# A seventh product taken in quarters, with eleven small sums on GpSimd, two passing weight quarters by DMA and half of C scaled last, in a Strassen matmul on one core

## The chip, the core and the metric

The kernel runs on one core of one Trainium2 chip. The metric is the device time of one execution in microseconds; the time before is the median of three runs, 1456.64 us (1456.58 to 1457.28). The profiled execution that the views come from has a span of 1455.0 us from its first to its last instruction.

## What is computed

```python
cs = np.cumsum(x, axis=1)                       # x: 8 x 2048 x 2048, w: 2048 x 2048, float32
diff = cs - np.concatenate([zeros, cs[:, :-1, :]], axis=1)
return np.matmul(diff, w)
```

The running sum and the difference undo each other, so the result is x times w: 16384 rows, in 128 row tiles of 128, by 2048 columns.

## The kernel before

**Stages.** Row tiles 0 to 3 are done plainly while w arrives (lines 180 to 457). Tiles 4 to 7 (`group_plain`, L628) and 8 to 11 (`group_half`, L752) lead over to the steady part: 29 groups of four row tiles, g, h, k and l (class `Group`, L957), from tile 12 on. A group multiplies its four tiles with all of w by a Winograd form of Strassen's scheme: the four tiles make a 2 x 2 block of A (rows g, h above k, l; each tile has a left and a right half of the inner dimension), w a 2 x 2 block of B, and seven products P1 to P7 give the four blocks of C. Weights stay in SBUF as f16, with their sums T1 to T4 (`T3 = B22 - B12`).

**Products.** P1 to P5 are each taken by the same scheme a second time, as seven quarter products p1 to p7: a quarter is four matmuls of 128 x 512 (L573), so such a product is 28 matmuls. P6 (S2 x T2) and P7 (S3 x T3) are taken whole, by `whole` (L1182) and `steps` (L547), 32 matmuls each at L554. A group is 5 x 28 + 2 x 32 = 204 matmuls.

**What surrounds a quarter product.** Four small sums of x halves per product, s1 to s4 (`small_sums`, L1001, `total` at L544, 128 x 512 f16 on VectorE; s1 feeds s2, s2 feeds s4). Eight sums S1 to S4 of whole tiles (128 x 1024, L544 too). Some weight quarters have no place in SBUF and pass through one buffer, `flow`: `fill_by` (L934) has VectorE compute a quarter (128 x 2048 f16, L937) just before the product that reads it, six times a group (P1.fp4, P2.fp4, P3.fp2, P4.fp4, P5.fp4, P5.fp5). PSUM has eight banks; `copy` (L1023, ScalarE) and `merge` (L1030, VectorE, `PSUM bank = PSUM bank + c`) carry a partial sum from one bank to others.

**C.** Each result piece of 128 x 512 f32 is started in an SBUF buffer c (seven of them, list `free`) by `keep` (L581, ScalarE: `c = bank * unit`) and completed by `add` (L584, VectorE: `c = bank * unit + c`), then stored by `put` (L595, a DMA of SyncE). A group has 16 keeps, 26 adds and 16 puts.

**x.** A row tile is loaded in two halves (L111), its absolute sum taken (`weigh`, ScalarE, L123), turned into a scale and its inverse (`scale_of`, VectorE, L139 and L141; `unit_of`, GpSimd, L147, 128 x 1), narrowed to f16 in place (L158, ScalarE) and transposed by DMA (L171). Left halves rotate through three buffers `F[:, 0..2]`, right halves through two.

**Order.** Every instruction is put behind the one before it on its engine (`after`, L86), and the order is written out in `ORDER` (L1195): one round of 188 steps for a group in the steady state, where `+1` and `+2` mean steps of the next groups. So each engine works through its own steps strictly in the order of that text. `END_ORDER` (L1227) orders P4 of the last group.

Of the kernel before, what the change touches and what calls it, by code (L numbers as in the profile page):

```python
# [10 lines left out]
def kernel(  # L11
# [86 lines left out]
    for t in range(PLAIN + 4, END, 4):  # L98
        queue_of_x += [t, t + 2, t + 1, t + 3]
    for i, t in enumerate(queue_of_x):  # L100
        where[t] = [F[:, i % 3, :], F[:, 3 + i % 2, :]]
# [30 lines left out]
    def scale_of(t):  # L132
        if t < END:
# [6 lines left out]
            )  # L140
            after("dve", lambda: nc.vector.reciprocal(s, m))  # L141
            sizes[t] = m

    def unit_of(t):
        if t < END:
            u, m = unit[t], sizes.pop(t)
            after("pool", lambda: nc.gpsimd.tensor_scalar(u, m, uw, None, MUL))  # L147
# [346 lines left out]
    class Inner:  # L494
# [20 lines left out]
        def weights(self):  # L515
# [4 lines left out]
            return {j: pieces_of(t) for j, t in places.items()}  # L520
# [10 lines left out]
    def half_of(t, i):  # L531
        return in_twos(t)[:, i]
# [10 lines left out]
    def total(dst, p, q, op):  # L543
        after("dve", lambda: nc.vector.tensor_tensor(dst.all, p.all, q.all, op))  # L544
# [389 lines left out]
    def fill_by(op, a, b):  # L934
        def some():
            x, y = (in_twos(t) for t in (a, b))
            after("dve", lambda: nc.vector.tensor_tensor(in_twos(flow), x, y, op))  # L937

        return some

    sevens = {
        "P1": (in_1, {"p4": fill_by(SUB, quarter_of(0, 1, 0), S1_all)}),
        "P2": (in_2, {"p4": fill_by(SUB, quarter_of(4, 1, 0), inner[:, 8:12, :])}),
        "P3": (in_3, {"p2": fill_by(ADD, spare_of(2, 0), inner[:, 16:20, :])}),
        "P4": (in_4, {"p4": fill_by(SUB, quarter_of(7, 1, 0), spare_of(2, 4))}),
# [3 lines left out]
                "p4": fill_by(SUB, quarter_of(1, 1, 0), quarter_of(6, 1, 0)),  # L949
                "p5": fill_by(SUB, quarter_of(1, 1, 1), quarter_of(6, 1, 0)),  # L950
# [5 lines left out]

    class Group:  # L957
        def __init__(self, g):
            self.tiles = dict(g=g, h=g + 2, k=g + 1, l=g + 3)
# [26 lines left out]
        def quarter(self, P, j, b, fresh):  # L986
# [4 lines left out]
            def some():  # L991
                to, a = self.bank(b, fresh), self.sums[P][j]
                quarter(
                    to, self.real(a), passed if j in passes else inner.weights()[j], fresh
                )
# [5 lines left out]
        def small_sums(self, P, a, b, dead, places=()):  # L1001
# [5 lines left out]
            def one(j, p, q, op):  # L1007
                if isinstance(to[j], str):
                    self.take(to[j], scratch)
                total(self.real(to[j]), self.real(p), self.real(q), op)  # L1010
# [37 lines left out]

        def row(self, c):
            return self.tiles[c[3] if c[1] == "1" else {"g": "k", "h": "l"}[c[3]]]  # L1050

        def keep(self, c, b, let=False):
            def some():
                keep(self.take(c, free), self.at[b], unit[self.row(c)])
# [231 lines left out]
```

## Time and profile before

| | before |
|---|---|
| median of runs | 1456.64 us |
| span of the profiled execution | 1455.0 us |
| busy: PE / VectorE (DVE) / ScalarE (ACT) / GpSimd (POOL) | 1441.1 / 1333.3 / 967.5 / 48.6 us |
| one group in the steady state | 44.03 us |
| DVE, ACT and POOL busy in it | 40.78, 29.6 and 1.07 us |

The runs' time has 1.6 us around the span. A busy time is the union of an engine's instructions, so where two of them overlap by their ends it is less than the sum of their durations. PE is matmul, PEld weight loads (beside PE), SP is SyncE, whose queue issues all DMAs of the steady part. A releaser ("<-") is what an engine's idle time before an instruction ended with.

### The profile page before, as it was taken

What the parts mean: (1) busy time and instruction counts of PE and PEld (TensorE: products, weight loads), DVE (VectorE), ACT (ScalarE), POOL (GpSimd) and SP (SyncE); (2) the same over time, 40 slices, a digit from 0 to 9 for tenths busy, and PEclk for the clock granted to TensorE, in tenths of its full rate; (3) what the DMA queues carried; (4) which work ended last, traced back from release to release, by engine and by line L of the source; (5) the groups of instructions that cost most, each with busy time, mean ns of one, the idle gap of its engine ahead of it and who ended that gap; (6) DMA issues with size and microseconds to landing.
All of it is one profiled execution on the core that took longest, in us unless ns stands there. A gap on an engine that the chain in (4) does not pass through costs nothing.

```text
span 1455.0 us, 20120 instructions
## 1 busy us (share of the span) xinstructions
PE 1441.1 (99%) x6673; PEld 652.6 (45%) x6679; DVE 1333.3 (92%) x2302; ACT 967.5 (66%) x1446; POOL 48.6 (3%) x136
## 2 busy tenths in 40 slices
PE   8999999999999999999999999999999999999998
PEld 3444444444444444444444444444444444444443
DVE  7998899999999999999999999999999999999998
ACT  5887656676666666667666667766666766666662
POOL 0111000000000000000000000000000000000000
PEclk9999999999999999999999999999999999999999
DMA  9999868898888998878998888998878898888983
GB/s 360 367 240 299 236 171 234 248 246 232 234 237 237 248 253 230 235 236 233 260 241 233 231 228 240 260 238 241 225 235 247 247 233 239 226 244 246 253 203 123
DMA packets 377752, 351.59 MB, mean 242 GB/s; under 512 B 274800, under 2 KB 274800, under 8 KB 377520
## 3 DMA queue, kind: packets, MB, share of 16 engines
q1 hardware_dynamic: 377088, 348.47, 84.9%
q0 software_dynamic: 560, 1.84, 0.3%
q8 instruction: 52, 0.85, 0.2%
q14 instruction: 52, 0.43, 0.1%
HBM read 150.99 MB, written 134.22 MB: 196 GB/s over the span
## 4 chain that ended last, share of the span: by engine, by line
PE 96%; DMA 2%; DVE 1%; issue 0%; ACT 0%; SPq 0%; DVEq 0%; ACTq 0%
PE b L573 61%; PE b L554 32%; PE b L275 2%; DMA W<-in_w_dram 1%; DMA W<-in_x_dram 1%; DVE c L584 1%; ACT wb L259 0%; PE b L400 0%; DVE x L544 0%; SPq L219 0%; DVE b L1030 0%; DVE flow L937 0%; DVE inner L544 0%; DVE W L541 0%; ACT c L581 0%
## 5 line engine op out<-in xcount | busy, mean ns | idle before, releaser
L584 DVE SCALAR_TENSOR_TENSOR c<-b,of,c 128x512 f32<-128x512 f32 x790 | 574.1, 747 | 74.3 <-PE b L573 64.3
L554 PE MATMUL b<-W,x 128*128 128x512 f16 x2144 | 506.6, 379 | 0.0
L581 ACT ACTIVATE c<-b,of 128x512 f32<-128x512 f32 x492 | 312.6, 680 | 230.9 <-PE b L573 113.3
L573 PE MATMUL b<-W,x 128*128 128x512 f16 x1892 | 452.4, 379 | 0.8 <-ACT b L1023 0.7
L158 ACT ACTIVATE F<-F,of 128x1024 f16<-128x1024 f32 x246 | 282.2, 1147 | 174.8 <-DVE of L141 172.6
L573 PEld LDWEIGHTS <-x 128*128 128x128 f16 x2488 | 243.4, 98 | 295.3 <-issue 2.7
L554 PEld LDWEIGHTS <-x 128*128 128x128 f16 x2144 | 209.8, 98 | 253.0 <-DVE x L544 0.2
L123 ACT ACTIVATE waste<-F 128x1024 uint8<-128x1024 f32 x246 | 259.3, 1054 | 4.6 <-DMA F<-in_x_dram 2.5
L573 PEld LDWEIGHTS <-inner 128*128 128x128 f16 x1648 | 161.2, 98 | 195.6 <-issue 1.3
L573 PE MATMUL b<-W,inner 128*128 128x512 f16 x944 | 242.2, 379 | 0.9 <-DVE b L1030 0.9
L544 DVE TENSOR_TENSOR x<-x,x 128x1024 f16<-128x1024 f16 (+1 forms) x388 | 226.6, 584 | 3.3
L573 PE MATMUL b<-flow,x 128*128 128x512 f16 x588 | 150.9, 379 | 0.0
L573 PE MATMUL b<-inner 128*128 128x512 f16 x472 | 121.1, 379 | 0.0
L937 DVE TENSOR_TENSOR flow<-W 128x2048 f16<-128x2048 f16 x87 | 105.8, 1216 | 0.0
L1030 DVE TENSOR_TENSOR b<-b,c 128x512 f32<-128x512 f32 x116 | 80.6, 695 | 13.9 <-PE b L573 13.9
L147 POOL TENSOR_SCALAR of<-of,uw 128x1 f32<-128x1 f32 x124 | 43.6, 370 | 1306.7 <-DVE of L139 704.1
L937 DVE TENSOR_TENSOR flow<-W,inner 128x2048 f16<-128x2048 f16 x58 | 70.8, 1220 | 0.0
L1023 ACT COPY c<-b 128x512 f32<-128x512 f32 x58 | 33.4, 576 | 51.3 <-PE b L573 51.3
L275 PE MATMUL b<-wb,xP 128*128 128x512 bf16 x234 | 57.0, 395 | 5.3 <-ACT wb L259 3.9
L544 DVE TENSOR_TENSOR inner<-x 128x512 f16<-128x512 f16 x117 | 49.4, 422 | 2.9 <-DMA x<-F 0.9
L1023 ACT COPY b<-b 128x512 f32<-128x512 f32 x87 | 51.2, 588 | 0.5 <-PE b L573 0.5
L544 DVE TENSOR_TENSOR inner<-x,inner 128x512 f16<-128x512 f16 x117 | 49.2, 421 | 2.0
(67 smaller groups left out, 530.0 us busy)
## 6 DMA issues: line engine op xcount, KB each, us to landing
F<-in_x_dram SPq DMA_DIRECT2D x246, 512.0 KB, 5.1
out_dram<-c SPq DMA_DIRECT2D x492, 256.0 KB, 3.0
W<-in_w_dram SPq DMA_DIRECT2D x32, 512.0 KB, 9.6
W<-in_x_dram SPq DMA_DIRECT2D x16, 256.0 KB, 7.2
x<-F SPq DMA_TRANSPOSE x246, 3.4
out_dram<-o POOLq DMA_DIRECT2D x5, 256.0 KB, 4.1
out_dram<-o SPq DMA_DIRECT2D x5, 256.0 KB, 3.5
xP<-in_x_dram SPq DMA_DIRECT2D x1, 1024.0 KB, 5.1
```

Of the source, the lines that this page charges most:

```text
L123: lambda: nc.scalar.activation(waste, where[t][i], ABS, scale=1.0 / ROW, accum_out=sums_of[t][:, i : i + 1],),
L147: after("pool", lambda: nc.gpsimd.tensor_scalar(u, m, uw, None, MUL))
L158: lambda: nc.scalar.activation(narrowed(t)[:, ds(i * NH, NH)], where[t][i], COPY, scale=s),
L275: lambda: nc.tensor.matmul(ps[r][n], xP[:, r, ko, :], wb[h, ko][:, ds(n * NB, NB)], start=(ko == 0), stop=(ko == KO - 1),),
L544: after("dve", lambda: nc.vector.tensor_tensor(dst.all, p.all, q.all, op))
L554: said = nc.tensor.matmul(to[n], a[k], b[k][:, n, :], start=(first and k == 0), stop=(k == KH - 1), skip_group_check=True,)
L573: said = nc.tensor.matmul(to, a[k], b[k], start=(first and k == 0), stop=(k == 3), skip_group_check=True)
L581: after("act", lambda: nc.scalar.activation(c, p, COPY, scale=u))
L584: after("dve", lambda: nc.vector.scalar_tensor_tensor(c, p, u, c, MUL, ADD))
L937: after("dve", lambda: nc.vector.tensor_tensor(in_twos(flow), x, y, op))
L1023: after("act", lambda: nc.scalar.copy(c, p))
L1030: after("dve", lambda: nc.vector.tensor_tensor(t, p, s, ADD))
```

## The change

- **P7 by seven quarter products** (`onto`), on top of what P6 left in the four banks x: four copies (c1, c5, c6, c7) on ScalarE and six merges (a1, a5g, a5h, a6, a7h, a7k) on VectorE take its partial sums to the banks, three of its weight quarters pass by fills (P7.fp4, P7.fp5, P7.fp7), and it has four small sums. T3's own quarters are rewritten once at the start (`sums_of_T3`).
- **Eleven of the now 24 small sums** go to GpSimd (`ON_POOL`).
- **Two of the now nine fills** (P1.fp4 and P5.fp5) are computed once by VectorE, stored to a DRAM tile and from the next group on loaded from there by a DMA of SyncE (class `Fill`), into the third left buffer of x, which the x tiles give up after the first eleven.
- **Eight of 16 result pieces** (`LATE`; not in the last group) are kept without their factor, added as a plain tensor_tensor, and scaled in place at the end by ScalarE (`last.*`).
- The reciprocal is a step of its own (`recip`), and `ORDER` is a new text.

```diff
+    THREE = 11
     for i, t in enumerate(queue_of_x):
-        where[t] = [F[:, i % 3, :], F[:, 3 + i % 2, :]]
+        j = i % 3 if i < THREE else (i - THREE) % 2
+        where[t] = [F[:, j, :], F[:, 3 + i % 2, :]]
...
+    ON_POOL = "P1.s1 P1.s4 P2.s1 P2.s2 P2.s3 P3.s2 P3.s3 P4.s2 P4.s3 P4.s4 P5.s2".split()
+    def total(dst, p, q, op, pool=False):
+        if pool:
+            after("pool", lambda: nc.gpsimd.tensor_tensor(dst.all, p.all, q.all, op))
+        else:
+            after("dve", lambda: nc.vector.tensor_tensor(dst.all, p.all, q.all, op))
...
+    flows = [flow, F[:, 2, :].bitcast(f16).rearrange("p (k n) -> p k n", k=4)]
+    class Fill:
+        def __call__(self):
+            if self.again is not None:
+                after("sp", lambda: nc.sync.dma_start(self.to, self.again))
+                return
+            x, y = (in_twos(t) for t in (self.a, self.b))
+            after("dve", lambda: nc.vector.tensor_tensor(in_twos(self.to), x, y, self.op))
+            if self.can:
+                self.again = kept.tile([P, 4, NB], f16, name=f"kept{len(stored)}")
+                stored.append(self)
+                after("sp", lambda: nc.sync.dma_start(self.again, self.to))
...
+        "P7": (
+            in_7,
+            {
+                "p4": Fill(SUB, quarter_of(5, 1, 0), quarter_of(5, 0, 1)),
+                "p5": Fill(SUB, quarter_of(5, 1, 1), quarter_of(5, 0, 1)),
+                "p7": Fill(SUB, quarter_of(5, 0, 1), quarter_of(5, 0, 0)),
+            },
+        ),
...
+    LATE = 'C12g0 C12g1 C12h1 C12h0 C11g1 C11h1 C21g1 C21h1'.split()
...
+        def onto(self, P, h0, h1, g0, g1):
+            q, e = f"{P}q", f"{P}e"
+            self.quarter(P, "p1", q, True)
+            self.step(f"{P}.c1", snap(f"{P}1", q))
+            self.merge(f"{P}.a1", g0, g0, f"{P}1", let=True)
+            self.quarter(P, "p2", g0, False)
+            self.quarter(P, "p5", e, True)
+            self.step(f"{P}.c5", snap(f"{P}5", e, True))
+            self.merge(f"{P}.a5g", g1, g1, f"{P}5")
+            self.merge(f"{P}.a5h", h1, h1, f"{P}5", let=True)
+            self.quarter(P, "p3", g1, False)
+            self.quarter(P, "p6", q, False)
+            self.step(f"{P}.c6", snap(f"{P}6", q))
+            self.merge(f"{P}.a6", g1, g1, f"{P}6", let=True)
+            self.quarter(P, "p7", q, False)
+            self.step(f"{P}.c7", snap(f"{P}7", q, True))
+            self.merge(f"{P}.a7h", h1, h1, f"{P}7")
+            self.merge(f"{P}.a7k", h0, h0, f"{P}7", let=True)
+            self.quarter(P, "p4", h0, False)
...
         def keep(self, c, b, let=False):
+                if c in self.late:
+                    after("act", lambda: nc.scalar.copy(to, p))
+                else:
+                    keep(to, p, u)
         def add(self, c, b, tag, let=False):
+                if c in self.late:
+                    after("dve", lambda: nc.vector.tensor_tensor(to, p, to, ADD))
+                else:
+                    add(to, p, u)
         def put(self, c):
+            if c in self.late:
+                self.step(f"last.{c}", lambda: keep(self.at[c], self.at[c], unit[self.row(c)]))
...
-            self.whole("P7", T3, half["g"][0], half["h"][0], *x)
+            self.small_sums("P7", A("g", 0), A("h", 0), True)
+            self.onto("P7", *x)
...
+    ORDER = """
+    P5.p7+0 P5.m2+0 P4.p2+0 P3.p6+0 keep.C22h1+0 P3.s3+0 P5.p3+0 put.C22g0+0 P5.fp4+0
+    P5.p4+0 add.C12h1.z+0 scale.h+1 add.C12g1.q+0 keep.C12h0+0 keep.C22h0+0 P7.a7k+0
+    P4.p1+0 recip.h+1 P4.s1+0 P7.fp4+0 keep.C21g0+0 P3.p7+0 turn1.g+1 put.C12g0+0
+    add.C21g0.x+0 P4.s3+0 P3.p4+0 P7.p4+0 P1.fp4+1 P1.p1+1 load.k+1 add.C12h1.q+0
+    narrow0.h+1 keep.C22g1+0 add.C12h0.z+0 add.C22g1.x+0 P3.p3+0 turn0.h+1 unit.g+1
+    P4.s2+0 add.C12h0.q+0 add.C22h0.x+0 add.C12g1.z+0 narrow1.h+1 P1.cg+1 turn1.h+1
+    P4.p6+0 last.C12h0+0 weigh0.k+1 P4.fp4+0 weigh1.k+1 P4.s4+0 add.C22h1.x+0 scale.k+1
+    recip.k+1 P3.p5+0 add.C12g1.e+0 put.C22h0+0 P4.p5+0 P4.p3+0 P1.p2+1 narrow0.k+1
+    P1.s1+1 add.C12h1.e+0 P1.s2+1 P4.p4+0 P1.p5+1 P1.s3+1 last.C12h1+0 keep.C21h1+0
+    put.C21g0+0 put.C22g1+0 keep.C21g1+0 put.C12h0+0 P1.s4+1 P1.ct+1 P1.p6+1 P2.p1+1
+    add.C21h1.e+0 add.C21g1.q+0 put.C22h1+0 narrow1.k+1 P1.m1+1 add.C21g1.x+0 P2.s1+1
+    P2.s2+1 load.l+1 keep.C11g0+1 unit.h+1 P2.cv+1 turn0.k+1 P4.p7+0 add.C21h1.q+0
+    last.C12g1+0 P2.fp4+1 P1.p7+1 P2.s4+1 P1.p3+1 P2.p2+1 P1.m2+1 P2.s3+1 P2.p6+1
+    weigh0.l+1 P1.p4+1 keep.C11g1+1 weigh1.l+1 add.C11g0.v+1 keep.C21h0+0 add.C11g1.q+1
+    scale.l+1 recip.l+1 narrow0.l+1 P2.p5+1 turn1.k+1 S1.g+1 narrow1.l+1 put.C11g0+1
+    S2.g+1 P2.p7+1 add.C21h0.x+0 put.C12g1+0 keep.C11h1+1 add.C11h1.q+1 P5.p1+1
+    turn0.l+1 last.C21g1+0 P6g.0+1 P6g.3+1 add.C11h1.e+1 S4.g+1 turn1.l+1 P2.p4+1
+    keep.C11h0+1 add.C11h0.q+1 P5.cg+1 P3.fp2+1 put.C21g1+0 last.C11h1+1 P6g.2+1
+    last.C21h1+0 S1.h+1 S2.h+1 P5.p2+1 put.C21h0+0 unit.k+1 P6g.1+1 P2.p3+1 put.C12h1+0
+    load.g+2 put.C21h1+0 keep.C22g0+1 keep.C12g0+1 S3.g+1 S4.h+1 P5.s1+1 P5.s2+1 P3.p2+1
+    add.C11g1.e+1 add.C12g0.z+1 last.C11g1+1 P6h.1+1 P5.s3+1 P6h.0+1 P6h.3+1 P5.s4+1
+    weigh0.g+2 P6h.2+1 weigh1.g+2 P5.fp5+1 P7.p1+1 P7.c1+1 P7.fp5+1 S3.h+1 P7.s1+1
+    put.C11h0+1 scale.g+2 P7.s3+1 recip.g+2 narrow0.g+2 keep.C12g1+1 P5.p6+1 P7.a1+1
+    P7.s2+1 P7.p5+1 P7.c5+1 P7.fp7+1 P7.s4+1 P5.p5+1 put.C11h1+1 put.C11g1+1 P7.a5g+1
+    P3.s1+1 P7.p6+1 P7.p2+1 keep.C12h1+1 P7.c6+1 P7.p7+1 unit.l+1 P7.a6+1 P5.ct+1
+    load.h+2 P7.a5h+1 turn0.g+2 P7.p3+1 add.C22g0.x+1 P3.s2+1 P7.c7+1 narrow1.g+2
+    P3.p1+1 P5.m1+1 P3.s4+1 weigh0.h+2 P7.a7h+1 add.C12g0.q+1 last.C12g0+1 weigh1.h+2
+    """
+    def sums_of_T3():
+        less(in_7.t12, in_7.t12, in_7.t11)
+        less(in_7.Q2, in_7.t22, in_7.t12)
```

95 lines of the change are left out of this document (43 added, 52 removed).

## The prediction

> **What bounds the kernel now.** I read the page first (busy times and the chain that ended last), then the table by windows for two rounds of the steady part, then the chain in order of time, then the groups.
>
> ```profile
> PE 1441.1 (99%) x6673; PEld 652.6 (45%) x6679; DVE 1333.3 (92%) x2302; ACT 967.5 (66%) x1446; POOL 48.6 (3%) x136
> ...
> PE 96%; DMA 2%; DVE 1%; issue 0%; ACT 0%; SPq 0%; DVEq 0%; ACTq 0%
> ```
>
> ```profile
> core 0: us, PE busy (x) PEld busy (x) DVE busy (x) ACT busy (x) POOL busy (x), PEclk, DMA share, GB/s
> ...
> 822.63:866.66 44.03, 44.03 (x206) 19.98 (x204) 40.78 (x72) 29.60 (x46) 1.07 (x4) 1.00 0.87 238
> ...
> 1350.99:1395.02 44.03, 44.03 (x206) 19.95 (x204) 40.79 (x72) 29.61 (x46) 1.07 (x4) 1.00 0.89 239
> ```
>
> ```profile
> 1350.99 18.13 PE b L573 x84
> ...
> 1395.02 18.13 PE b L573 x84
> ```
>
> The chain is matmul for 96% of the span. Equal places of two rounds lie 44.03 us apart (1350.99 and 1395.02), 84 matmuls in a row take 18.13 us, so one takes 0.2158 us, and the group's 204 matmuls take 204 x 0.2158 = 44.03 us: PE loses nothing in a round. The granted clock is 1.00, so there is nothing to win from it. Next comes VectorE with 40.78 us of 44.03, 93%; 3.25 us of its round are idle. ScalarE has 14.4 us free and GpSimd 43.
>
> What ends VectorE's idle time in that round, from the list of waits of 822.63 to 866.66:
>
> ```profile
> ACT F L158 <- DVE of L141: 5.9, 3, 2.8
> ...
> DVE c L584 <- PE b L573: 2.1, 5, 0.8
> ...
> DVE b L1030 <- PE b L573: 0.5, 1, 0.5
> ```
>
> 2.6 of its 3.25 us are waits for PE: VectorE had caught up with the matmuls. Such idle time is slack, and it shrinks by itself when VectorE has more to do. The 5.9 us in which ScalarE's narrowing waits for the reciprocal (L141) is a block at the head of an engine that works in order.
>
> **The change, part by part.**
>
> *Matmuls.* P7 goes from 32 to 28, a group from 204 to 200: 200 x 0.2158 = 43.16 us, 0.863 less. 29 groups: **-25.0 us**. That is certain as work and is also the most that can be won: 1455.0 - 25.0 = 1430.0 us of span. The median of the runs is 1.6 us above the span, so 1431.6.
>
> *VectorE's work per group.* The prices, from the groups by shape, and below them the same instructions in order of time:
>
> ```profile
> L584 DVE SCALAR_TENSOR_TENSOR c<-b,of,c 128x512 f32<-128x512 f32 x790 | 574.1, 747 | 74.3 <-PE b L573 64.3 <-ACT c L581 1.3
> ...
> L937 DVE TENSOR_TENSOR flow<-W 128x2048 f16<-128x2048 f16 x87 | 105.8, 1216 | 0.0
> L1030 DVE TENSOR_TENSOR b<-b,c 128x512 f32<-128x512 f32 x116 | 80.6, 695 | 13.9 <-PE b L573 13.9
> ...
> L544 DVE TENSOR_TENSOR inner<-x 128x512 f16<-128x512 f16 x117 | 49.4, 422 | 2.9 <-DMA x<-F 0.9
> ```
>
> ```profile
> 834.63 0.74 DVE L584 SCALAR_TENSOR_TENSOR c<-b,of,c 128x512 f32<-128x512 f32 x1
> 835.29 0.69 DVE L1030 TENSOR_TENSOR b<-b,c 128x512 f32<-128x512 f32 x1
> 835.89 1.22 DVE L937 TENSOR_TENSOR flow<-W,S 128x2048 f16<-128x2048 f16 x1
> 837.02 0.42 DVE L544 TENSOR_TENSOR inner<-x 128x512 f16<-128x512 f16 x1
> 837.48 0.42 DVE L544 TENSOR_TENSOR inner<-inner,x 128x512 f16<-128x512 f16 x1
> 837.82 0.69 DVE L1030 TENSOR_TENSOR b<-b,c 128x512 f32<-128x512 f32 x1
> ```
>
> The starts show what an instruction really takes from the round, since its end lies over the next one: an add 835.29 - 834.63 = 0.66, a merge 0.60, a fill 1.13, a small sum 0.34 (837.48 to 837.82) to 0.46 when the next one needs it (837.02 to 837.48), 0.40 on average. I use these, and the full durations as the other end:
> - six merges more: 6 x 0.60 = +3.6 (full: 6 x 0.695 = +4.2)
> - fills 6 to 7 (nine, less two by DMA): +1.13 (+1.22)
> - small sums 20 to 13 (24, less eleven): -7 x 0.40 = -2.8 (-2.95)
> - 18 of the 26 adds belong to late pieces and become plain tensor_tensor. The trace has that form only into PSUM, the merge: -18 x 0.06 = -1.1 if it costs the same into SBUF, 0 if it costs what the add does. I take -1.0, since the merge has the same operation and the same two kinds of input.
>
> Sum +0.9, so **41.7 us** busy in a round of 43.16 (41.2 with the other ends in its favour, 43.3 with all against, just over the matmuls): 97%, with 1.5 us free instead of 3.25. Without the three parts that take work off VectorE (GpSimd, DMA, late scaling) it would be 41.7 + 11 x 0.40 + 2 x 1.13 + 1.0 = 49.4, and VectorE the bound by far.
>
> *ScalarE.* Four copies more, and eight scalings of a c; the eight late keeps become copies. From the groups:
>
> ```profile
> L581 ACT ACTIVATE c<-b,of 128x512 f32<-128x512 f32 x492 | 312.6, 680 | 230.9 <-PE b L573 113.3 <-issue 63.2 <-PE b L554 28.6
> ...
> L1023 ACT COPY c<-b 128x512 f32<-128x512 f32 x58 | 33.4, 576 | 51.3 <-PE b L573 51.3
> ```
>
> +4 x 0.58 + 8 x 0.68 - 8 x 0.10 = +6.9 us: 36.5 of 43.16, 85%. It hides beside the matmuls, but a late scaling waits for VectorE's last add, and what stands behind it on ScalarE waits too: behind `last.C12h1` stand keep.C21h1, keep.C21g1 and P1.ct, and P1.ct feeds the merge P1.m1. 6.6 us of free time has to cover such blocks and the 5.9 us of the reciprocal's.
>
> *GpSimd.* Eleven sums of 128 x 512. No instruction of the trace shows that size on GpSimd; these are the bounds:
>
> ```profile
> 78.86 1.36 POOL L147 TENSOR_SCALAR of<-of,uw 128x1 f32<-128x1 f32 x1 [4.79 <-DVE of L139]
> ...
> 116.86 0.28 POOL L147 TENSOR_SCALAR of<-of,uw 128x1 f32<-128x1 f32 x1 [5.01 <-DVE of L139]
> ...
> 139.70 1.90 POOL L147 TENSOR_SCALAR of<-of,uw 128x1 f32<-128x1 f32 x1 [16.29 <-DVE of L139]
> ```
>
> Between 0.28 us (128 x 1) and 1.90 us (the longest GpSimd instruction beside VectorE's work). I take the upper one, as the work is 512 times that of the row: 11 x 1.9 = 21 us of 43, still half free. The four `unit` steps queue behind the sums and have no waiter in the list of waits. What counts is not GpSimd's time but what its sums do to VectorE, below. The Trainium skill, "GPSIMD Engine Reference", section "3.1 Elementwise — side-by-side cycle accounting", gives 2.6 cycles an element at 1.2 GHz: by it a sum would be an estimated 1.1 us and eleven 12 us, and no run here shows it.
>
> *The two fills by DMA.* 2 x 512 KB per group, issued by SyncE ahead of the x loads (P1.fp4 stands before load.k).
>
> ```profile
> 0.00:50.00 50.00, 43.20 (x205) 19.71 (x210) 39.18 (x43) 33.35 (x38) 0.19 (x4) 1.00 0.97 373
> ```
> ```profile
> F<-in_x_dram SPq DMA_DIRECT2D x246, 512.0 KB, 5.1
> ```
>
> While w arrives, 373 GB/s fill 0.97 of the queues: 1.05 MB is 2.7 us of them. A round has 0.87 x 44.03 = 38.3, and 41.0 of 43.16 is 95%. In the text 64 matmuls (13.8 us) lie between P1.fp4 and P1.p4, 12 (2.6 us) between P5.fp5 and P5.p5, against 5.1 us to landing of a load of that size. But SyncE's queue holds nothing between put.C21h1 and P5.fp5, and from that store on it is 32 matmuls, 6.9 us; so I cost both at nothing. The x tiles' left halves drop from three buffers to two, as the right halves have had all along without any wait for a load in the round; nothing again.
>
> *Start and end.* The two sums for T3 at the start are 2 x 1.2 = +2.4 us of VectorE. The last group ends with P4 as before.
>
> *Sum.* 1430.0 + 2.4 = 1432.4, and for the thinner cover I allow 0.15 us of PE idle per group, a tenth of VectorE's free 1.5 us (my choice; the round before loses none): 29 x 0.15 = 4.4. Span 1436.8, and with 1.6 around it **1438 us**.
>
> **The rivals.**
>
> *VectorE becomes the bound and keeps its idle time* (slower). 41.7 + 3.25 = 44.95 a round: 29 x 0.92 = +27 us, **1483**. It decides from 44.03 - 41.7 = 2.3 us of idle time on; below 1.5 PE stays the bound. For it: seven fills go through the one buffer `flow`, each between two quarter products, so VectorE has to be in time for each; three sums now make a round trip to GpSimd in mid-chain (P1.s1, P1.s4, P5.s2). Against: 2.6 of the 3.25 us are waits of a VectorE that was early. Chance 0.20.
>
> *GpSimd and VectorE exclude each other* (slower). Beside these GpSimd rows VectorE ran:
>
> ```profile
> 78.88 3.68 DVE L457 TENSOR_TENSOR W<-W 128x1024 f16<-128x1024 f16 x6
> ...
> 116.88 0.75 DVE L584 SCALAR_TENSOR_TENSOR c<-b,of,c 128x512 f32<-128x512 f32 x1
> ```
>
> Beside sums of two SBUF operands the same small GpSimd instruction took 1.36 instead of 0.28 us; beside an add that reads PSUM it did not. Every trace row shows GpSimd the loser; whether VectorE loses as well when GpSimd is first, no row shows. If so, a sum on GpSimd holds back the fill or sum of two SBUF operands behind it. In the new order seven of eleven stand beside adds and merges (P4.s2 beside three adds), four beside or just before such operands: P3.s3 by P5.fp4, P1.s4 by P1.s3, P2.s2 by P2.fp4, P5.s2 by P5.s3. Four times the hold of the row, 1.36 - 0.28 = 1.08, is 4.3 us: 41.7 + 4.3 = 46.0 a round, 29 x 2.0 = +57, **1514**. Chance 0.12. The Trainium skill, "SBUF — State Buffer", section "Who interferes with whom", has it as a rule: an instruction of VectorE with two SBUF inputs and one of GpSimd that reads SBUF exclude each other, and the second one is blocked for the whole of the first. The trace agrees for the one direction (1.36 against 0.28).
>
> *The cheap add isn't cheaper* (the change doesn't do all it says). VectorE 42.7, 0.45 us free; half of 1.5 - 0.45 lost by PE, 29 x 0.5 = 15: 1434 + 15 = **1449**. Chance 0.09.
>
> *Fills land late.* Two fills late by 0.43 us each take back the 0.86 of a round: **1457**. For it: 6.9 us at most for P5.fp5 against 5.1, and a store before it that waits for a late scaling; against: the buffer is free long before. Chance 0.04.
>
> **How the numbers follow.** PE stays the bound: 0.55, 1431 to 1446, 1438. The rivals have 0.20, 0.12, 0.09 and 0.04. About 0.2% of the time, 2.9 us, is what a measurement of this kernel can tell from no change. Faster: 0.55 + 0.09 = 0.64. Same: the late fills, 0.04. Slower: 0.20 + 0.12 = 0.32. The range leaves out the GpSimd rival and a little of the VectorE one: 1430 (the floor less what a profile may differ) to 1488.
>
> **What would show it.** PE windows: a round of 43.2 to 43.4 us with the idle time in front of few matmuls. VectorE near 41.7 busy in it; the late add near 0.695 us. If VectorE is the bound, PE's waits name L544, the fill's line or L1030 as releaser, and the chain shows them by turns. If the two exclude each other, sums and fills of 0.42 and 1.22 us come out longer beside a GpSimd row, or start late with GpSimd as the releaser. Late fills would show as matmuls waiting for a DMA. Wrong it would be above all if VectorE's idle time stays over 2.3 us a round.

## The result and the profile after

The changed kernel takes **1497.54 us** (median of four runs, 1494.42 to 1498.95) against 1456.61 us for the kernel before: 1.0278 times as long, 95% interval 1.0263 to 1.0292. The prediction was 1438 us, and its range ended at 1488. The span of the profiled execution is 1495.5 us, its mean granted clock 0.997, against 0.999 before.

The page of the kernel after, its busy times and its chain:

```profile
PE 1441.7 (96%) x6557; PEld 638.1 (43%) x6563; DVE 1357.4 (91%) x2306; ACT 1162.9 (78%) x1786; POOL 475.2 (32%) x455
...
DVE 42%; PE 24%; DMA 18%; ACT 7%; issue 6%; SPq 2%; POOL 0%; ACTq 0%; DVEq 0%; POOLq 0%
```

Before, the chain was 96% matmul. Now it goes through five things by turns, and none of them is busy all the time. Here are 21 rounds of the steady part, between two equal places, in the table by windows (columns as before: PE, PEld, DVE, ACT, POOL busy, clock, DMA share, GB/s):

```profile
451.59:1399.96 948.37, 925.04 (x4202) 409.03 (x4201) 868.81 (x1512) 766.14 (x1197) 330.40 (x316) 1.00 0.97 256
```

A round takes 948.37 / 21 = 45.16 us. The matmuls need 43.16, so 2.0 us are lost in each. VectorE is busy for 41.37 us of it, ScalarE for 36.5, GpSimd for 15.7. VectorE's idle time is 45.16 - 41.37 = 3.8 us, more than the 3.25 of before. Of the 40.5 us by which the span grew, 29 x (45.16 - 44.03) = 32.8 come from the rounds and 7.7 from the start and the end.

The waits of those 21 rounds (us in total, times, longest), POOL's left out:

```profile
PEld L586 <- issue: 53.7, 130, 1.5
ACT c L594 <- DVE c L1137: 42.8, 61, 2.2
DVE c L1137 <- ACT c L1126: 40.1, 42, 1.9
...
ACT c L1126 <- DMA out_dram<-c: 25.6, 23, 3.0
...
ACT c L594 <- DMA out_dram<-c: 16.6, 17, 2.5
...
DVE c L1137 <- ACT c L594: 14.1, 21, 0.7
...
ACT c L1064 <- DMA out_dram<-c: 7.3, 10, 1.4
PE b L586 <- DVE c L1137: 6.4, 21, 1.0
...
PE b L586 <- DMA F<-kept: 4.8, 9, 1.2
...
DVE c L597 <- PE b L586: 3.3, 11, 0.5
PE b L586 <- DVE b L1071: 3.0, 6, 0.6
```

L1126 is the copy with which a late piece starts, L1137 its plain add, L594 a keep or the late scaling, L1064 the copies for P1, P2 and P5, L597 an add with its factor, L1071 a merge, L586 a quarter's matmul. VectorE hardly waits for PE any more: all its waits for PE in the 21 rounds are 4.3 us. It waits for ScalarE, (40.1 + 14.1) / 21 = 2.6 us a round. ScalarE waits for VectorE, and for stores that give a buffer c back: (25.6 + 16.6 + 7.3) / 21 = 2.4 us. Before, no wait of ScalarE for a store stands in its list. PE's loss is spread over some six places a round (130 / 21) at which its weight loads stand with "issue", that is, with no releaser that the profile shows. At some of them the matmuls' own waits name one: a plain add (6.4 us), a reload (4.8) or a merge (3.0). For the others it stays open what PE waits for.

VectorE's own list in order of time shows two of its waits in a round:

```profile
495.97 1.29 DVE L1137 TENSOR_TENSOR c<-b,c 128x512 f32<-128x512 f32 x2 [1.08 <-ACT c L1126]
...
506.23 1.42 DVE L1137 TENSOR_TENSOR c<-b,c 128x512 f32<-128x512 f32 x2 [0.87 <-ACT c L1126]
```

and ScalarE's list what stood ahead of the two copies for which the first one waited:

```profile
494.25 0.72 ACT L594 ACTIVATE c<-c,of 128x512 f32<-128x512 f32 x1
494.88 1.05 ACT L1126 COPY c<-b 128x512 f32<-128x512 f32 x2
```

The scaling `last.C12h1` runs first, then keep.C21h1 and keep.C21g1, then the adds onto them. DMA issues, size and median us to landing, which were 5.1 and 3.0 before:

```profile
F<-in_x_dram SPq DMA_DIRECT2D x246, 512.0 KB, 6.4
out_dram<-c SPq DMA_DIRECT2D x492, 256.0 KB, 4.2
F<-kept SPq DMA_DIRECT2D x56, 512.0 KB, 5.2
```

One count shows how a store comes to be waited for. ScalarE's groups of the kernel after:

```profile
L594 ACT ACTIVATE c<-b,of 128x512 f32<-128x512 f32 x268 | 180.9, 680 | 97.9 <-PE b L586 35.4 <-DVE of L150 21.6 <-DMA out_dram<-c 19.5
...
L1126 ACT COPY c<-b 128x512 f32<-128x512 f32 x224 | 127.1, 576 | 38.3 <-DMA out_dram<-c 32.0 <-PE b L586 3.9 <-DVE b L1071 2.1
...
L1096 ACT COPY c<-b 128x512 f32<-128x512 f32 x116 | 67.8, 584 | 29.4 <-PE b L586 27.4 <-DMA out_dram<-c 1.3
...
L1064 ACT COPY c<-b 128x512 f32<-128x512 f32 x58 | 34.6, 596 | 11.9 <-DMA out_dram<-c 9.3 <-PE b L586 2.0
```

All of these take a c from the same seven. Before there were 16 keeps and 58 / 29 = 2 copies a round, 18 uses; P7 in quarters adds 116 / 29 = 4. So a use may last 7 x 44.03 / 18 = 17.1 us before and 7 x 43.16 / 22 = 13.7 us at the speed that the change was to have. And each late piece holds its c longer, by its scaling, and each store by 1.2 us.

### The profile page after: what moved, and what is told of

The parts are those of the page before. It is cut to its first block, busy times and chain, and to the rows that moved or that the text cites. A ratio compares the mean times of both kernels' runs of the same rounds, so it can differ in the third digit from the quotient of the medians.

```text
span 1495.5 us, 21083 instructions
## 1 busy us (share of the span) xinstructions
PE 1441.7 (96%) x6557; PEld 638.1 (43%) x6563; DVE 1357.4 (91%) x2306; ACT 1162.9 (78%) x1786; POOL 475.2 (32%) x455
## 4 chain that ended last, share of the span: by engine, by line
DVE 42%; PE 24%; DMA 18%; ACT 7%; issue 6%; SPq 2%; POOL 0%; ACTq 0%; DVEq 0%; POOLq 0%
PE b L586 14%; DVE c L1137 12%; DVE b L1071 8%; PE b L567 8%; DMA F<-in_x_dram 7%; DVE flow L963 7%; DVE c L597 6%; DMA out_dram<-c 6%; DVE x L557 4%; DVE inner L557 3%; DMA x<-F 2%; PE b L283 2%; ACT c L594 2%; DMA W<-in_w_dram 2%; ACT c L1126 2%
## 5 line engine op out<-in xcount | busy, mean ns | idle before, releaser
L586 PE MATMUL b<-W,x 128*128 128x512 f16 x2124 | 517.5, 379 | 16.4 <-DVE c L1137 8.6
L586 PEld LDWEIGHTS <-x 128*128 128x128 f16 x2952 | 287.1, 97 | 399.2 <-issue 65.7
L1137 DVE TENSOR_TENSOR c<-b,c 128x512 f32<-128x512 f32 x504 | 332.9, 682 | 75.0 <-ACT c L1126 52.2
L586 PEld LDWEIGHTS <-inner 128*128 128x128 f16 x1996 | 194.8, 98 | 254.5 <-issue 14.3
L586 PE MATMUL b<-W,inner 128*128 128x512 f16 x1176 | 297.9, 380 | 0.8 <-DVE b L1071 0.7
L567 PE MATMUL b<-W,x 128*128 128x512 f16 x1216 | 282.7, 379 | 0.0
L125 ACT ACTIVATE waste<-F 128x1024 uint8<-128x1024 f32 x246 | 258.5, 1051 | 24.0 <-DMA F<-in_x_dram 21.4
L555 POOL TENSOR_TENSOR inner<-inner,x 128x512 f16<-128x512 f16 x87 | 101.4, 1166 | 532.0 <-DMA out_dram<-c 239.9
L594 ACT ACTIVATE c<-b,of 128x512 f32<-128x512 f32 x268 | 180.9, 680 | 97.9 <-PE b L586 35.4
L597 DVE SCALAR_TENSOR_TENSOR c<-b,of,c 128x512 f32<-128x512 f32 x286 | 210.2, 742 | 13.4 <-PE b L586 9.6
L555 POOL TENSOR_TENSOR x<-x,x 128x512 f16<-128x512 f16 x116 | 160.5, 1384 | 190.7 <-DVE x L557 188.4
L594 ACT ACTIVATE c<-c,of 128x512 f32<-128x512 f32 x224 | 158.7, 720 | 58.9 <-DVE c L1137 57.8
L1071 DVE TENSOR_TENSOR b<-b,c 128x512 f32<-128x512 f32 x290 | 197.0, 688 | 5.9 <-ACT c L1096 2.8
L586 PE MATMUL b<-flow,x 128*128 128x512 f16 x704 | 180.5, 378 | 5.7 <-ACT c L1096 2.0
L1126 ACT COPY c<-b 128x512 f32<-128x512 f32 x224 | 127.1, 576 | 38.3 <-DMA out_dram<-c 32.0
L586 PE MATMUL b<-inner 128*128 128x512 f16 x472 | 121.1, 379 | 0.6 <-DVE c L597 0.6
L555 POOL TENSOR_TENSOR inner<-x 128x512 f16<-128x512 f16 x58 | 82.3, 1419 | 35.7 <-DMA x<-F 30.5
L1096 ACT COPY c<-b 128x512 f32<-128x512 f32 x116 | 67.8, 584 | 29.4 <-PE b L586 27.4
```

The source lines that it names most:

```text
L125: lambda: nc.scalar.activation(waste, where[t][i], ABS, scale=1.0 / ROW, accum_out=sums_of[t][:, i : i + 1],),
L555: after("pool", lambda: nc.gpsimd.tensor_tensor(dst.all, p.all, q.all, op))
L567: said = nc.tensor.matmul(to[n], a[k], b[k][:, n, :], start=(first and k == 0), stop=(k == KH - 1), skip_group_check=True,)
L586: said = nc.tensor.matmul(to, a[k], b[k], start=(first and k == 0), stop=(k == 3), skip_group_check=True)
L594: after("act", lambda: nc.scalar.activation(c, p, COPY, scale=u))
L597: after("dve", lambda: nc.vector.scalar_tensor_tensor(c, p, u, c, MUL, ADD))
```

## The experiments

All times are medians, and all ratios stand against the kernel before. Letters of theories are explained in each expectation.

**Is it a part that could be undone?** The first four undo one part each in the order of after.

e1: the two weight quarters aren't loaded again.

```diff
             if self.again is not None:
-                after("sp", lambda: nc.sync.dma_start(self.to, self.again))
                 return
```

> The two fills that pass by DMA are not loaded again after the first group: their products read whatever lies in the buffer, so those two quarter products get wrong weights; everything else stays. Theory A (the two loads of 512 KB a group fill the DMA queues, 0.97 of the round; stores land in 4.2 instead of 3.0 us, the seven buffers c come free late, ScalarE's keeps and copies wait for a store, VectorE's adds for ScalarE, PE for VectorE): the round goes from 45.2 to 43.2-43.6 us, the time to 1432-1450. Theory B (VectorE, 41.4 us busy, is the bound with the idle time that its order leaves, whatever the DMA does): 1485-1500. Theory C (GpSimd and VectorE exclude each other): 1485-1500, nothing of it is touched.

1494.09 us, 1.0258 (1.0241 to 1.0275). The DMA share of the steady part falls from 0.97 to 0.90, the time by 3.4 us. In this order of steps these transfers are not the cause, and theory A fell. The stores still land in 4.2 us, so the two transfers aren't what lengthened them either.

e2: these two fills by VectorE in each round again.

```diff
-            if self.can:
+            if False:
```

> The same two fills computed by VectorE each time, as before the change, in the same buffers. VectorE gets 2 x 1.13 = 2.3 us a round more (41.4 to 43.7), the DMA 1.05 MB less. Theory A: the waits for stores go, and VectorE with 43.7 plus 0.5 to 1 of idle is the bound: a round of 44.2-44.7, the time 1465-1485, faster than the changed kernel in spite of more work on VectorE. Theory B or C: 2.3 us a round on top of 45.2, the time near 1497 + 65 = 1560.

1546.25 us, 1.0615 (1.0599 to 1.063), between what the theories gave.

e3: all small sums on VectorE.

```diff
-    ON_POOL = "P1.s1 P1.s4 P2.s1 P2.s2 P2.s3 P3.s2 P3.s3 P4.s2 P4.s3 P4.s4 P5.s2".split()
+    ON_POOL = []
```

> All 24 small sums on VectorE. 11 x 0.40 = 4.4 us a round more there (41.4 to 45.8 less what the exclusion costs now). Theory C: with GpSimd out of the way VectorE loses its hidden blocks, and the time is at or below the changed kernel's, 1480-1500. Theory A: VectorE is now the bound at 45.8, the DMA's waits partly beside it: a round of 46-48.5, the time 1525-1590. Theory B: 45.2 + 4.4 = 49.6, the time 1625.

1566.21 us, 1.0765 (1.0733 to 1.0797), in the range of theory A, though A had fallen with e1. Two fills are 29 x 2 x 1.13 = 66 us of VectorE and cost 49 us; eleven sums are 29 x 11 x 0.40 = 128 us and cost 69. In this order both parts are worth having.

e4: no late scaling.

```diff
-    LATE = 'C12g0 C12g1 C12h1 C12h0 C11g1 C11h1 C21g1 C21h1'.split()
+    LATE = []
```

> No piece of C is scaled late: all 16 keeps with their factor, all 26 adds with it, no scaling at the end. ScalarE loses 8 x 0.72 us and gains 8 x 0.10, 36.5 to 31.6 a round; VectorE gains 18 x 0.06 = 1.1, 41.4 to 42.4. A store can start right after its last add, so a buffer c comes free about 1 to 2 us earlier. Theory A: still waits for stores, a little fewer: 1485-1510. Theory D (the late scalings block ScalarE's queue, and that is the loss): 1455-1480. Theory B: +1.1 a round, 1530.

1500.62 us, 1.0303 (1.028 to 1.0327). That is 3.1 us more than with it, but the runs overlap (1497.05 to 1505.4 against 1494.42 to 1498.95), so no difference is shown. Its groups show where ScalarE's saving went:

```profile
L594 ACT ACTIVATE c<-b,of 128x512 f32<-128x512 f32 x492 | 326.3, 681 | 198.1 <-DMA out_dram<-c 90.3 <-PE b L586 78.7 <-PE b L567 7.6
```

ScalarE has no scalings to do and waits 90.3 us for stores instead. The edit does two things at once: ScalarE is busy for 1043.6 instead of 1162.9 us, and VectorE, whose adds have their factor again, for 1393.1 instead of 1357.4. So it shows that both together are no relief in this order, and not what the scaling alone costs here.

e7: P7 in quarters alone, with none of the three parts that take work off VectorE (the edits of e2, e3 and e4 together).

> P7 by seven alone, in the changed order: all sums and all nine fills on VectorE, no late scaling. VectorE's work is 41.4 + 3.4 + 2.3 + 1.2 = 48.3 us a round (the three by the runs that undid one each); with 2.8 us of idle 51.1, the time 1457 + 29 x 7.1 = 1660. If it comes out much lower, the hiding parts cost more than the work that they take away.

1610.83 us, 1.106 (1.1038 to 1.1082). That is 44.03 + (1610.83 - 1456.6) / 29 = 49.3 us a round; the prediction had 49.4 of VectorE's work for this case. Between 500 and 1400 us VectorE is busy for 877.3 of 900 us, 48.1 us of such a round, so the work was 1.3 us less than the prediction had and idle time makes up the rest: that the two numbers meet is partly luck. The expectation of this run, 1660 us, was 49 us too high. By its own words the three parts then cost more than the work that they take away: together they take 1541.9 - 1357.4 = 184.5 us off VectorE and win 113 us of time.

**GpSimd beside VectorE.** e5: its sums of 8 columns instead of 512.

```diff
-            after("pool", lambda: nc.gpsimd.tensor_tensor(dst.all, p.all, q.all, op))
+            after("pool", lambda: nc.gpsimd.tensor_tensor(dst.all[:, :8], p.all[:, :8], q.all[:, :8], op))
```

> GpSimd's eleven sums take 8 of 512 columns, so that their results are mostly not computed; each still starts and ends in its place. It takes away GpSimd's time (1.2 to 2.1 us a sum) and what it holds up in VectorE. Theory C: VectorE's sums and fills get shorter and the time falls by 20 us or more, to 1455-1477. Theory E or B: GpSimd's sums were waited for by nothing much, 1488-1497.

1488.99 us, 1.0226 (1.0209 to 1.0243), 8.5 us less, so theory C's 20 us or more fell. VectorE's sums, first in the kernel after, then in e5:

```profile
L557 DVE TENSOR_TENSOR inner<-x,inner 128x512 f16<-128x512 f16 x117 | 54.3, 464 | 1.0 <-POOL inner L555 1.0
...
L557 DVE TENSOR_TENSOR x<-x,x 128x512 f16<-128x512 f16 x61 | 28.5, 468 | 0.1
```

```profile
L557 DVE TENSOR_TENSOR inner<-x,inner 128x512 f16<-128x512 f16 x117 | 49.0, 419 | 0.0
...
L557 DVE TENSOR_TENSOR x<-x,x 128x512 f16<-128x512 f16 x61 | 25.3, 417 | 0.1
```

VectorE does lose beside GpSimd, 54.3 + 28.5 - 49.0 - 25.3 = 8.5 us in these two groups, 0.3 us a round and not 4.3; its other sums and its fills keep their durations. Single rows of the kernel after show how:

```profile
711.55 1.22 DVE L963 TENSOR_TENSOR flow<-W 128x2048 f16<-128x2048 f16 x1
711.71 2.07 POOL L555 TENSOR_TENSOR x<-x,x 128x512 f16<-128x512 f16 x1 [6.59 <-DVE x L557]
```

```profile
906.73 1.38 DVE L557 TENSOR_TENSOR inner<-x,inner 128x512 f16<-128x512 f16 x1
```

The GpSimd sum starts inside a fill and ends 1.01 us after the fill's end, where an undisturbed one takes 1.15 us in all. VectorE's sum starts inside a GpSimd sum (906.52 to 907.82) and ends 0.29 us after that one's end, so it takes 1.38 instead of 0.42 us. All 28 of VectorE's small sums that take more than 0.5 us start inside a GpSimd sum and end 0.27 to 0.29 us after it. So whichever starts second waits for the end of the first, in both directions. It costs little because VectorE comes second only about once a round, and in 22 of the 28 cases the GpSimd sum has less than 0.3 us to go.

That the time falls by 8.5 us as well needn't be this alone. In e10, below, 102 us less of VectorE's work win only 18 us, and e5 also has GpSimd's own sums ready earlier.

**The order of ScalarE's steps.** e8 puts the three steps for which VectorE's regular waits stood in line behind the keeps: `last.C12h1` behind keep.C21g1, `narrow1.l` behind keep.C11h1, `last.C12g0` and `weigh1.h` behind keep.C22h1.

```diff
-    P1.s1+1 add.C12h1.e+0 P1.s2+1 P4.p4+0 P1.p5+1 P1.s3+1 last.C12h1+0 keep.C21h1+0
-    put.C21g0+0 put.C22g1+0 keep.C21g1+0 put.C12h0+0 P1.s4+1 P1.ct+1 P1.p6+1 P2.p1+1
+    P1.s1+1 add.C12h1.e+0 P1.s2+1 P4.p4+0 P1.p5+1 P1.s3+1 keep.C21h1+0
+    put.C21g0+0 put.C22g1+0 keep.C21g1+0 last.C12h1+0 put.C12h0+0 P1.s4+1 P1.ct+1 P1.p6+1 P2.p1+1
```

> Only ScalarE's order changes, in three places: last.C12h1 goes behind keep.C21h1 and keep.C21g1, narrow1.l behind keep.C11h1, last.C12g0 and weigh1.h behind keep.C22h1. In each of these places VectorE waits in every round for a keep that stands behind them on ScalarE: 1.08, 0.87 and 0.67 us, 2.6 of its 3.8 us of idle time. Theory E (since theory A fell: ScalarE hands VectorE its pieces late, because it works in order and stands at a late scaling or a narrowing; the round is a loop through both): the three waits shrink to 0.4, 0 and 0, the round to 43.3-44.2 us, the time to 1440-1468. Theory B (idle time is a matter of the whole tight order and comes back elsewhere): 1485-1497. Theory C (exclusion): no change, 1495.

1515.66 us, 1.0406 (1.0378 to 1.0433): 18 us **worse**, and above what any of the theories gave. VectorE's waits for L1126 halved (39.0 to 20.9 us between 500 and 1400 us), and others came in their place. In e8, for the same stretch:

```profile
ACT c L1126 <- DMA out_dram<-c: 34.4, 40, 2.7
...
DVE of L141 <- ACT waste L125: 25.3, 43, 1.2
...
ACT c L594 <- DVE b L1071: 20.5, 19, 1.1
```

ScalarE's copies wait longer for stores (24.8 us in the kernel after). The other two waits come from the move itself. keep.C22h1 (L594) waits 1.1 us in almost every round for a merge of VectorE, and `weigh1.h` (L125), which now stands behind it, is late for the scale (L141) by 0.74 us:

```profile
942.34 0.21 DVE L141 TENSOR_SCALAR of<-of 128x1 f32<-128x1 f32 x1 [0.74 <-ACT waste L125]
```

That wait is there once a round and makes up 14.8 of the 25.3 us. e9 is the same without the reloads:

> The three moves and no reloading of the two passing quarters (their products read what lies in the buffer). If, once ScalarE's keeps are in time, the DMA is the next thing late (theory A as the second limit), this is 15-40 us below the run with the moves alone; if not, within 5 us of it.

1495.03 us, 1.0271 (1.0248 to 1.0294): in this order the reloads cost 20 us, in the other 3.4. The waits named for e8 stand in e9 too (L141 for L125 28.9 us, the keeps for a merge 22.2, the copies for stores 30.5), at a time only 0.9 us above e1. So they are not enough to explain e8's 18 us, and through which wait the reloads cost more in this order isn't shown. My theory that three blocks at the head of ScalarE made the loss fell: moving them moves the waits.

**One relief at a time.** Each of these takes something off one engine or gives one kind of buffer more room. e10, fills over one of two column halves:

```diff
-            after("dve", lambda: nc.vector.tensor_tensor(in_twos(self.to), x, y, self.op))
+            after("dve", lambda: nc.vector.tensor_tensor(in_twos(self.to)[:, :1], x[:, :1], y[:, :1], self.op))
```

> Every fill by VectorE computes half of its quarter (two of four blocks; the other half stays as it was). VectorE's work falls by 7 x 0.53 = 3.7 us a round, 41.4 to 37.7; nothing else changes. The three undoings gave 0.7 us of time per us of VectorE's work. Theory B (VectorE limits the round over most of its length): 29 x 0.7 x 3.7 = 75 us less, no lower than the matmuls, 1432-1450. Theory E or F (ScalarE's work, or c buffers and x buffers that come free late, limit it): above 1470.

1479.39 us, 1.0156 (1.0141 to 1.0171). VectorE is busy for 1255.2 instead of 1357.4 us, 102 less, and the time falls by 18. Theory B, VectorE as the limit of most of the round, fell.

e11, the absolute sum of x over half of the columns:

```diff
-                        waste,
-                        where[t][i],
+                        waste[:, :NB],
+                        where[t][i][:, :NB],
```

> The absolute sums are taken over half of each x half (a smaller norm; the scale cancels in the result). ScalarE's work falls by 8 x 0.43 = 3.4 us a round, 36.5 to 33.1, and each scale is known 0.9 us earlier. Theory E (ScalarE hands its pieces on late because it is too full to make up for a block): 1440-1465. Theory B: its blocks are short beside VectorE's work, 1480-1495.

1483.19 us, 1.0179 (1.0164 to 1.0194): 14 us for 103 us less of ScalarE (1060.2 instead of 1162.9). Theory E, a ScalarE that is too full, fell.

e12, the two passing quarters read from a resident one, and the buffer used for two more c; e13, the same buffer given back to x instead:

```diff
-            self.to = flows[again]
+            self.to = quarter_of(5, 1, 0) if again else flow
...
-            if self.again is not None:
-                after("sp", lambda: nc.sync.dma_start(self.to, self.again))
+            if self.can:
                 return
...
+    free += [F[:, 2, :NB], F[:, 2, NB:]]
```

> The two passing quarters are neither filled nor loaded; their products read another quarter that lies in SBUF. The freed 4 KB become two more buffers c, nine instead of seven. To be set against the run that only leaves out the reloading, 1494. Theory G (the late pieces and the four copies of P7 hold buffers c longer, and ScalarE's keeps wait for a store to land, 2.4 us a round): 1440-1470. Theory B: 1485-1495.

> As the run with nine buffers c, but the freed 4 KB are the third left buffer of x again, in all of the kernel. Theory X (with two left buffers a load waits for the transposes of the tile before last, lands late, and weigh, scale and narrow come late): 1440-1470. Theory B: 1485-1495.

1482.70 (1.0177, 1.0161 to 1.0192) and 1485.37 us (1.0188, 1.017 to 1.0205). To be compared with e1, which has no reload either: two c are worth 11.4 us, the third x buffer 8.7 (its four runs spread from 1481.68 to 1488.35). Theories G and X, each of which made its buffers most of the loss, fell. With nine c a use may last 9 x 43.16 / 22 = 17.7 us, and ScalarE's waits for stores are gone; the idle time before L1126, which is L1125 here, falls from 38.3 to 2.4 us:

```profile
L1125 ACT COPY c<-b 128x512 f32<-128x512 f32 x175 | 99.2, 576 | 2.4 <-DVE b L1070 1.8 <-PE b L586 0.7
```

e16, stores of half the columns:

```diff
-        after("sp", lambda: nc.sync.dma_start(out2[ds(t * P, P), ds(at * NB, NB)], c))
+        after("sp", lambda: nc.sync.dma_start(out2[ds(t * P, P), ds(at * NB, NB // 2)], c[:, : NB // 2]))
```

> The changed kernel with stores of 256 of the 512 columns of each result piece (half of C is left out): 128 KB instead of 256 KB per store, 2.1 MB less in a round, so the DMA share falls from 0.97 to about 0.80. Theory Q, the full DMA queues (x landing in 6.4 instead of 5.1 us, stores in 4.2 instead of 3.0) are what delays the round: 1475 us or less. Theory C: stores that end sooner free a c sooner, which is worth something like the two more c buffers, 1480 to 1490. If DMA has no part in it: 1494 or more, as without the reloads.

1473.27 us, 1.0116 (1.0101 to 1.0132): 24 us, the most of any single relief, and within what theory Q gave.

```profile
F<-in_x_dram SPq DMA_DIRECT2D x246, 512.0 KB, 5.9
out_dram<-c SPq DMA_DIRECT2D x492, 128.0 KB, 2.4
```

```profile
L1126 ACT COPY c<-b 128x512 f32<-128x512 f32 x224 | 126.2, 576 | 7.0 <-DMA out_dram<-c 4.0 <-DVE b L1071 2.1 <-PE b L586 0.8
```

A store gives its c back after 2.4 instead of 4.2 us, and the waits for stores go (32.0 to 4.0 us before this copy). It also takes more traffic away than e1 (share 0.84 against 0.90), so how much of the 24 is the c and how much the x loads, 5.9 instead of 6.4 us, isn't separated.

**Reliefs together.** e14 has the edits of e10 and e11, e15 those of e12 as well, e18 those of e16 as well.

> The changed kernel with two reliefs at once: the fills by VectorE compute one of their two column halves (the other half of a passing weight quarter is left over from before), and the absolute sum of x on ScalarE runs over 512 of its 1024 columns. Singly they gave 18 us (1479.4) and 14 us (1483.2). Theory C, one chain that goes in turn through all engines: what one relief wins is lost again at the next engine, so the two together give more than the sum of the two, under 1460 us. Theory D, each relief only takes away delays of its own and the rest of the loss sits elsewhere: the sum, 1497.5 - 18 - 14 = 1465, give or take 4. Theory S, both take away the same delays: 1475 or more.

> The same two reliefs and a third: the two weight quarters that come by DMA are read from a resident quarter instead (other numbers, no transfer), and the buffer that this frees holds two more result buffers c, nine instead of seven (singly, 1482.7). Theory C: matmuls bind again, 1432 to 1442 us. Theory D: 1465 - 15 = 1450. Theory S: 1470 or more.

> The changed kernel with all four reliefs: half of each VectorE fill, half of each absolute sum, no transfers for the two passing quarters with nine c, and stores of half the columns. Theory D, small delays that add up singly until the matmuls are reached: with three of them it was 1449.9, with the shorter stores 24 us less would be 1426, which the matmuls don't allow, so the floor of the sum, 1432 to 1437 us. If something else than these four still holds the round (the places at which PE waits just behind a step of another engine): 1442 or more.

| | us | ratio | sum of the single gains |
|---|---|---|---|
| e14, fills and absolute sum | 1469.79 | 1.0091 (1.0074 to 1.0108) | 1465 |
| e15, and nine c | 1449.86 | 0.9952 (0.9937 to 0.9967) | 1450 |
| e18, and short stores | 1438.67 | 0.9881 (0.9867 to 0.9896) | 1426, below the matmuls' floor |

The first three gains add: e15 wins 47.7 us where the single runs won 47.3. Within them e14 wins 4.7 us less than its sum and nine c on top of it 5.1 more, so the good sum is partly two deviations that cancel. The fourth can't be told by adding, because the matmuls' floor is 1430.0 of span, 2.4 for T3's sums and 1.6 around the span, 1434 us. Shorter stores win 24 us alone and 11 on top of the other three, with 16 to the floor. e18 stays 4.7 us above the floor and 1.7 above theory D's range. I had thought of one chain in which each relief only uncovers the next link and all together give much more than their sum; that fell. The chains of e15 and of e18:

```profile
PE 73%; DMA 13%; DVE 8%; ACT 3%; issue 2%; SPq 1%; POOL 0%; ACTq 0%; DVEq 0%; POOLq 0%
```

```profile
PE 92%; DMA 3%; ACT 2%; DVE 2%; issue 1%; SPq 0%; ACTq 0%; DVEq 0%
```

So no single one of these makes the loss. VectorE's work, ScalarE's work and the c with their stores each carry a part of it, and with all four reliefs the matmuls bind again: 58.9 of the 63.5 us above the floor are gone. Nine c and shorter stores are not two separate causes by these runs, since each of them takes away the same waits for stores. Whether each relief helps PE at places of its own isn't shown.

**The late scaling alone, on the kernel before.** e17 has it in the order of before, right ahead of each store; e19 the same without the scaling itself.

```diff
+    LATE = 'C12g0 C12g1 C12h1 C12h0 C11g1 C11h1 C21g1 C21h1'.split()
...
-                keep(self.take(c, free), self.at[b], unit[self.row(c)])
+                if c in self.late:
+                    after("act", lambda: nc.scalar.copy(to, p))
...
-                add(self.at[c], self.at[b], unit[self.row(c)])
+                if c in self.late:
+                    after("dve", lambda: nc.vector.tensor_tensor(to, p, to, ADD))
...
+                if c in self.late:
+                    keep(self.at[c], self.at[c], unit[self.row(c)])
                 put(self.at.pop(c), self.row(c), n)
```

> The kernel before with the late scaling alone: eight of 16 pieces kept without the factor, added plainly, scaled on ScalarE right ahead of their store, in the order of before, with no other part of the change. ScalarE has 6.6 us more in a round of 44.03, about 36 of it, and VectorE 1 us less. Theory E, ScalarE's blocks behind a late scaling are what costs, in any order: 1475 us or more. Theory C, a delay costs only where no engine has time left to catch up, and here PE's round is longer and VectorE has 4 us free: 1455 to 1463.

> The kernel before with the late pieces kept and added without the factor as in the run with late scaling alone (1536.1 us), but without the scaling itself: half of C is stored unscaled. ScalarE's extra eight instructions per round and what waits behind them are gone, the cheap copies and plain adds stay. Theory E, the scaling blocks ScalarE and with it what stands behind: 1453 to 1460 us, all of the 79 us gone. If the copies and plain adds themselves or their waits cost it: 1475 or more.

1536.06 us (1.0543, 1.0528 to 1.0559) and 1456.72 us (1.0002, 0.9992 to 1.0011). The copies and plain adds cost nothing; eight scalings, 8 x 0.71 = 5.7 us a round on an engine with 14 us free, cost 79 us. Theory C, a delay that is caught up, fell. The chain of e17 in order of time shows how:

```profile
801.18 0.76 DVE c L584
...
801.96 5.20 DMA out_dram<-c
...
807.24 0.59 ACT c L1026
...
810.80 1.23 ACT c L581 x2
812.05 3.06 DMA out_dram<-c
...
815.18 0.59 ACT c L1059
...
815.82 1.02 PE b L554 x4
```

An add ends, the piece's store lands 5.2 us later, only then does a copy (L1026) get a c; behind it on ScalarE stand a keep, two absolute sums and then two scalings (L581), whose store takes 3.1 us, and only then gets a later keep (L1059) its c, and PE the bank that it frees, after an idle 1.7 us. I read this as a ring through stores, seven c and ScalarE's order; no run gives this kernel more c to test it. In e17 the idle time of ScalarE's keeps and copies names stores, 46.6 + 21.9 + 11.8 us; the chain of e19 is the one of before, 96% matmul. The granted clock doesn't explain the loss: it is 0.98 in parts of e17 (300 to 600 and 1300 to 1500 us), but from 600 to 1300 us, where it is 1.00, there are 3087 matmuls against 3245 before, 5% fewer.

## Why the prediction was wrong

**The sizes.** All but one came out.
- *Matmuls*: 200 a group, as counted; the 0.863 us were won as work and lost again as waits.
- *VectorE*: 41.7 us a round forecast, 41.37 measured. (The upper end, 43.3 "with all against", has the small sums at 0.42 us, which is in VectorE's favour; at 0.34 it would be 43.8.) The plain add takes 682 ns against the 695 taken, so the rival of the add that isn't cheaper fell.
- *ScalarE*: 36.5 forecast, 36.5 measured.
- *DMA*: share 0.95 forecast, 0.97 measured, but of a longer round. In time of the queues that is 43.8 us a round against 41.0, more than the 43.16 of the matmuls, so the term was 2.8 us too small and only the share came out, by luck.
- *GpSimd*: 1.9 us a sum taken, about 1.2 to 1.4 measured in the mean, within the bounds:

```profile
L555 POOL TENSOR_TENSOR x<-x,x 128x512 f16<-128x512 f16 x116 | 160.5, 1384 | 190.7 <-DVE x L557 188.4
...
L555 POOL TENSOR_TENSOR inner<-inner,x 128x512 f16<-128x512 f16 x87 | 101.4, 1166 | 532.0 <-DMA out_dram<-c 239.9 <-DVE inner L557 220.0 <-PE b L586 69.7
```

The 1166 ns agree with the estimate of 1.1 us from the Trainium skill, "GPSIMD Engine Reference", section "3.1 Elementwise — side-by-side cycle accounting".

**The step that failed** is the sentence "Such idle time is slack, and it shrinks by itself when VectorE has more to do", and with it the 0.15 us of PE idle a group, where 2.0 us were lost. It holds only as long as VectorE waits for PE alone. In the new round it waits for ScalarE's copies and scalings, and its idle time grew from 3.25 to 3.8 us. The rival "VectorE becomes the bound and keeps its idle time" had the size, 44.95 us a round against 45.16, and the threshold of 2.3 us was passed; the size is luck. Its mechanism was not right: VectorE isn't the bound either, since 102 us less of its work win 18 us of the 63 above the floor.

**What stood in its place**, none of it in the sum:
- *Result buffers.* I counted engines and queues and never the seven c. They go from 18 to 22 uses a round while each use gets longer. Two more c win 11.4 us (e12 against e1). Shorter stores win 24 (e16), of which a part may be the x loads.
- *Landing times.* I took the landing of before, 3.0 us a store and 5.1 an x load; in the new order they are 4.2 and 6.4. The DMA share alone doesn't set them: they are 4.2 and 6.2 in e1 at a share of 0.90, and 3.7 and 6.2 in e7 at 0.81, where before has 3.0 and 5.1 at 0.87. What lengthens them in the new order stays open.
- *x buffers*, costed at "nothing again": 8.7 us (e13 against e1).
- *Work of VectorE and ScalarE.* Both were to hide beside the matmuls. 102 us less of VectorE's win 18 (e10), 103 us less of ScalarE's 14 (e11), so neither hides wholly.
- *ScalarE's blocks.* I named the keeps behind `last.C12h1` and let 6.6 us of free time cover them. Free time doesn't cover a block on an engine that works in order; a wait of VectorE of 1.08 us or more for just these keeps is in every round. Putting the keeps first won nothing, though (e8 and e9).
- *Start and end*: 7.7 us instead of 2.4; the cause is open.

**The rivals.** *Mutual exclusion of GpSimd and VectorE*, priced at 57 us, is there as a mechanism, and its price was wrong: e5, which takes away what VectorE loses by it, wins 8.5 us. The prediction had four holds of 1.08 us a round; the trace has about one, mostly of 0.14 us. The Trainium skill, "SBUF — State Buffer", section "Who interferes with whom", has the second of the two blocked for the whole of the first. The trace agrees, and in both directions: the rows under e5 have a GpSimd sum of 2.07 us behind a fill and a sum of VectorE of 1.38 us behind a GpSimd sum. The means hide it, since VectorE's sums are only 45 to 51 ns longer in the mean. *Late fills*: 4.8 us of waits for F<-kept in 21 rounds, and 3.4 us of time.

The argument that the parts taken off VectorE are needed was right (e7: 49.3 us a round). Left open: whether another order of the same steps comes near the floor. The one other order that was tried was worse, and no version here beats the kernel before with the whole computation.

## What to carry over

Free time in a table of busy times is a reserve only for delays that the same engine may make up; before you spend it, look at what its waits would end with in the new order, and count the rotating buffers (uses a round, the time each use is held, stores included) as you count engines. A round in which PE and the queues are busy for 97% or more, VectorE for 92% and ScalarE for 81% had no single bound to relieve: here three reliefs of 14 to 18 us added up, and it took a fourth to come near the matmuls' floor. A step moved in one engine's order moves the waits of all that stands behind it.

## What the runs showed of the hardware

- A store of 128 x 512 f32 lands in 3.0 us in the order of before (DMA share 0.87) and in 4.2 in the new one (0.97), still 4.2 at 0.90 (e1) and 3.7 at 0.81 (e7), so the share alone doesn't set it. One of half the size lands in 2.4 us (e16).
- The plain add PSUM + SBUF into SBUF takes 682 ns, into PSUM 688, with a factor per row 742.
- In the kernel after, the 28 small sums of VectorE that take more than 0.5 us instead of 0.42 all start inside a GpSimd sum and end 0.27 to 0.29 us after it. The GpSimd sum at 711.71, which starts inside a fill, ends 1.01 us after the fill.
- The late scaling of eight pieces, 5.7 us a round of a ScalarE with 14 us free, costs 79 us in the order of before (e17 against e19).
